# Layer 0, second half: weight buffers by place in SBUF, and the gate rows and residual loaded among the weights

## The chip, the core and the metric

The kernel runs on one core of one Trainium2 chip. TensorE (PE in the profile) multiplies, VectorE (DVE) and ScalarE (ACT) work elementwise, SyncE (SP) and GpSimd (POOL) issue the DMA transfers here. SBUF is the on-chip memory of 128 partitions in which every operand stands; PSUM takes the products. The metric is the device time of one execution in microseconds, as the median of several runs.

## The reference, cut to what matters

Two layers of a diffusion backbone over 256 context and 256 latent tokens of width 1024. A layer has a mixer (attention, SSD and retention side by side) and then a part that is called its second half here: an output projection with gated residual, a modulated RMSNorm, a squared-ReLU MLP and a gated residual. Layer 1 updates the latent tokens alone.

```python
def sq_relu_mlp(x, w1, w2):
    h = jax.nn.relu(x @ w1)          # 1024 -> 4096
    return (h * h) @ w2              # 4096 -> 1024

# merge_branches ends in: return merged @ w_out
for layer in range(DEPTH):
    mod_lat = jnp.split(jax.nn.silu(c) @ w_mod[layer] + b_mod[layer], 6, axis=-1)
    ...
    h_lat = h_lat + mod_lat[2][:, None, :] * mix_lat
    v_lat = modulate(rms_norm(h_lat, norm2_w[layer]), mod_lat[3], mod_lat[4])
    h_lat = h_lat + mod_lat[5][:, None, :] * sq_relu_mlp(v_lat, w_mlp1[layer], w_mlp2[layer])
    if need_ctx:                     # layer 0 alone: the same for the context tokens
        ...
```

All of it is in float32.

## The kernel before, in words

**Units.** A weight matrix is read in units of 128 x 1024 float32 (0.52 MB). For each, `load_w` takes a buffer `raw` and has SP load it, ScalarE casts it into `wh` (the leading part of the number, fp32r), and VectorE takes `wl = raw - wh` (`split`, under high priority). `fm` then runs 24 matmuls: for each of 8 slices of the contraction `wh` with the leading part of the activations, `wh` with their rest, and `wl` with the leading part. In layer 0 each streams 512 columns (the context and latent tokens), so a unit is 24 matmuls of 512 columns.

**Activations.** `uh` and `ul` hold the leading part and the rest of the input of the output projection and of the MLP's first matrix; they stand in pool `cp`, at the low addresses of SBUF (36 to 68 KB of a partition). The hidden layer of the MLP, `hh_` and `hl_`, stands in `hpool`, at the high addresses (142 to 206 KB).

**Weight buffers.** `wh` and `wl` come from two pools: two of each from `wp`, which follows the activations at the low addresses (86 to 103 KB), and two of each from a pool that the second half opens for itself (`wb`, from 119 KB up). `alt` takes them in turn: unit number n of the half (counted from 1) gets the pool's buffers when n is even and over 4, else `wp`'s. So four units can stand converted. The first half of layer 0 has no such second pool for `wh` and `wl` (its `w` is 0) and runs with the two of `wp` alone. `raw` has three buffers in `wp` and one in the pool.

**Order of the second half of layer 0.** Output projection: units wo0 to wo6, then wo7 in two halves of 256 columns with the norm behind each (`last_block`). Then MLP in two rounds of 16 units w1 and 16 units w2 (two for each of 8 output blocks); the first two w1 units of round one, and the last two w2 units of round two, run in halves of 256 columns. Behind each wo unit stands the residual of that block, which adds it to the old h: `h` is loaded for this in eight pieces of 0.26 MB from DRAM. The weights of the gate of the MLP's residual (`graw`, 16 pieces of 0.26 MB) are loaded in this stretch too, for the small matmuls after wo7; they lie where `hh_` will be.

**What sets the order.** The program is recorded in the order of the code; a scheduler then puts the instructions of each engine into a fixed order by dependencies and priorities. Each engine runs its list strictly in that order, and SP issues its transfers strictly in that order; a DMA waits until its buffer is free.

## Time and profile before

| | |
|---|---|
| median of three runs | 1469.29 us (1468.2 to 1469.41) |
| the profiled execution | 1468.76 us, of which its span is 1467.0 |
| TensorE | busy 1444.2 us, 98% of the span; mean granted clock 0.996 |
| VectorE, ScalarE | busy 1011.4 us (69%) and 666.0 us (45%) |
| second half of layer 0 | from 515.5 us of the span to about 951 |

Matmul records overlap, so the busy share of TensorE does not tell how dense the matmuls are; the distance between the starts of two units does. A stretch of the second half can be read from three things: how long its units take, on which engine TensorE waits, and what the DMA engines moved.

### The profile page before, as it was taken

The page shows a single profiled execution, that of the slowest core. Times are in us where ns is not written, and L with a number is a line of the kernel's source. Part 1 is how long each engine was busy: PE and PEld are TensorE (multiplying, and loading weights), DVE is VectorE, ACT ScalarE, POOL GpSimd, SP SyncE. Part 2 cuts the span into 40 slices and gives each one's busy share as a digit, 9 for nine tenths or more (in the row PEclk, how much of TensorE's full clock was granted, in tenths as well). Part 3 has the DMA queues.
Part 4 walks back from the last instruction along what each step waited for, and adds up shares of the span by engine and source line. Part 5 has one row for each costly group of instructions (what it writes and reads, how often), then busy time and mean ns, then how long its engine had stood idle before and what let it go on. Part 6 is the DMA issues. An engine that isn't in the chain of part 4 may idle for free.

```text
span 1467.0 us, 22934 instructions
## 1 busy us (share of the span) xinstructions
PE 1444.2 (98%) x8950; PEld 1243.9 (85%) x8950; DVE 1011.4 (69%) x2003; ACT 666.0 (45%) x1170; POOL 70.6 (5%) x134
## 2 busy tenths in 40 slices
PE   8999999999999979999999999999999999999997
PEld 6888877878888868888888888987988999999997
DVE  5778599588866756896456643697894886775664
ACT  4577567242322334432224322476762444663553
POOL 0000010000000020000001100000000020000000
PEclk9999999999999999999999999999999999999999
DMA  9511343455135482454445543241443456665551
GB/s 354 178 44 44 101 127 98 129 172 158 35 109 170 147 311 77 158 198 161 143 156 189 189 130 107 80 131 53 141 147 101 144 190 222 219 190 187 185 182 65
DMA packets 65085, 217.09 MB, mean 148 GB/s; under 512 B 7600, under 2 KB 10032, under 8 KB 64848
## 3 DMA queue, kind: packets, MB, share of 16 engines
q1 hardware_dynamic: 50960, 166.80, 34.5%
q0 software_dynamic: 14016, 48.83, 10.3%
q8 instruction: 70, 1.15, 0.3%
q14 instruction: 39, 0.32, 0.1%
HBM read 213.44 MB, written 2.16 MB: 147 GB/s over the span
## 4 chain that ended last, share of the span: by engine, by line
PE 88%; DVE 5%; DMA 4%; issue 2%; ACT 1%; SPq 0%; POOL 0%; DVEq 0%; POOLq 0%
PE gps L255 23%; PE gps L253 23%; PE gps L254 23%; PE mps L669 2%; PE mps L630 1%; PE mps L652 1%; DMA raw<-in_wk_dram 1%; DVE wl L223 1%; DMA raw<-in_ws_dram 1%; PE mps L952 1%; PE mps L954 1%; PE mps L953 1%; DMA h<-in_h_dram 1%; PE mps L766 1%; PE mps L976 1%
## 5 line engine op out<-in xcount | busy, mean ns | idle before, releaser
L222 ACT CAST wh<-raw 128x1024 fp32r<-128x1024 f32 (+1 forms) x284 | 297.7, 1050 | 577.3 <-PE gps L254 476.7
L223 DVE TENSOR_TENSOR wl<-raw,wh 128x1024 fp32r<-128x1024 f32 (+1 forms) x284 | 347.3, 1224 | 263.2 <-ACT wh L222 259.8
L253 PE MATMUL gps<-uh,wh 128*128 128x256 f32 (+1 forms) x1304 | 444.3, 341 | 7.0 <-ACT wh L222 6.5
L255 PE MATMUL gps<-uh,wl 128*128 128x256 f32 (+1 forms) x1304 | 444.1, 341 | 1.2 <-DVE wl L223 1.2
L254 PE MATMUL gps<-ul,wh 128*128 128x256 f32 (+1 forms) x1304 | 443.9, 341 | 0.0
L253 PEld LDWEIGHTS gps<-uh,wh 128*128 128x128 f32 x1304 | 246.9, 189 | 35.9 <-ACT wh L222 7.3
L255 PEld LDWEIGHTS gps<-uh,wl 128*128 128x128 f32 x1304 | 247.0, 189 | 29.8 <-DVE wl L223 2.8
L254 PEld LDWEIGHTS gps<-ul,wh 128*128 128x128 f32 x1304 | 247.1, 190 | 27.3 <-issue 0.9
L255 PE MATMUL gps<-hh__5379,wl 128*128 128x512 f32 (+1 forms) x272 | 103.5, 380 | 0.0
L253 PE MATMUL gps<-hh__5379,wh 128*128 128x512 f32 (+1 forms) x272 | 103.3, 380 | 0.0
L254 PE MATMUL gps<-hl__5380,wh 128*128 128x512 f32 (+1 forms) x272 | 103.2, 379 | 0.0
L216 DVE CUSTOM_DVE_ANT_0 mraw<-mraw,crow,cl 128x1024 f32<-128x1024 f32 x64 | 82.0, 1281 | 1.1
L253 PE MATMUL gps<-hh__11969,wh 128*128 128x256 f32 x256 | 72.3, 282 | 0.0
L255 PE MATMUL gps<-hh__11969,wl 128*128 128x256 f32 x256 | 72.2, 282 | 0.0
L254 PE MATMUL gps<-hl__11970,wh 128*128 128x256 f32 x256 | 72.1, 282 | 0.0
L1100 DVE SCALAR_TENSOR_TENSOR h<-gps,mod,h 128x256 f32<-128x256 f32 x48 | 21.8, 480 | 70.6 <-PE gps L255 70.6
L254 PE MATMUL gps<-brl,wh 128*128 128x512 f32 (+1 forms) x192 | 65.7, 342 | 0.0
L255 PE MATMUL gps<-brh,wl 128*128 128x512 f32 (+1 forms) x192 | 65.6, 342 | 0.0
L253 PE MATMUL gps<-brh,wh 128*128 128x512 f32 (+1 forms) x192 | 65.2, 340 | 0.0
L253 PEld LDWEIGHTS gps<-hh__5379,wh 128*128 128x128 f32 x272 | 51.2, 188 | 10.3
L254 PEld LDWEIGHTS gps<-hl__5380,wh 128*128 128x128 f32 x272 | 51.2, 188 | 10.2
L208 POOL DMA_DIRECT2D mraw<-in_wt_dram x62 | 33.4, 539 | 548.6 <-DVE mod L216 531.7
(325 smaller groups left out, 2355.4 us busy)
## 6 DMA issues: line engine op xcount, KB each, us to landing
raw<-in_ws_dram SPq DMA_DIRECT2D x280, 512.0 KB, 3.5
mraw<-in_wt_dram POOLq DMA_DIRECT2D x62, 512.0 KB, 3.6
mraw<-in_wm_dram SPq DMA_DIRECT2D x16, 512.0 KB, 9.9
graw<-in_wg_dram POOLq DMA_DIRECT2D x32, 256.0 KB, 8.0
R<-drow POOLq DMA_DIRECT2D x24, 256.0 KB, 4.4
h<-in_h_dram SPq DMA_DIRECT2D x16, 256.0 KB, 6.6
raw<-in_wk_dram SPq DMA_DIRECT2D x4, 544.0 KB, 4.9
crow<-in_cr_dram SPq DMA_DIRECT2D x1, 1024.0 KB, 10.9
```

Of the source, the lines that this page charges most:

```text
L208: (nc.sync if l == 0 and cb < 18 else nc.gpsimd).dma_start(raw, wt[WTI[l] + cb - WT0[l]])
L216: V.tensor_tensor_reduce(o, r, crow[:, v], 0.5, col(l, "bm")[:, cb:cb + 1], ALU.mult, ALU.add, mods[l][:, cb, v:v + 1])
L222: W["cp"] = A.copy(hi, src)
L223: return V.tensor_tensor(lo, src, hi.bitcast(F32), ALU.subtract)
L253: PE.matmul(ps, a, xh(k), start=start and k == 0, stop=False)
L254: PE.matmul(ps, a, xl(k), start=False, stop=False)
L255: W["mm"] = PE.matmul(ps, b, xh(k), start=False, stop=stop and k == K - 1)
L630: PE.matmul(ps[:, u * nk:u * nk + nk], qT_[:, 4 * g + j0 + u, i * 128:i * 128 + 128], kT_[:, g, x, 0:nk], start=x == 0, stop=x == 1)
L652: PE.transpose(pt[:, c * 128:c * 128 + 128], pr[:, c * 128:c * 128 + 128], ident)
L669: PE.matmul(po[64 * u:64 * u + 64, jp * 128:jp * 128 + 128], vt[:, c, 64 * g:64 * g + 64], pT[:, c, u], start=c == 0, stop=c == ncn - 1, t ...
L766: PE.matmul(ps[:, 0:256], xb[:, c, 256:384], xd, start=True, stop=True)
L1100: W["dv"] = V.scalar_tensor_tensor(h[:, i, a:b], ps[:, a - q0:b - q0], coef[:, i, v:v + 1], h[:, i, a:b], ALU.mult, ALU.add)
```

## The change

Three things are changed in the second half of layer 0. A unit's `wh` and `wl` come from `wp` alone (two sets) where it meets `uh` and `ul` (wo, w1), and from the second pool alone (two sets) where it meets `hh_` and `hl_` (w2); the same for the first projection of layer 1, by halves. The 16 gate pieces are issued by SP and no longer by GpSimd, two behind each wo unit, the last four behind wo6. The pieces of h are issued two ahead of wo0 and then one behind each of wo0 to wo5; this loop is written for both layers, while the gate pieces of layer 1 stay as they were.

```diff
-        def load_w(src, n, pool=None):
+        def load_w(src, n, pool=None, far=False):
...
                 raw = alt("raw", F32, "r", 3)
-                wh = alt("wh", F32R, "w", 2)
-                wl = alt("wl", F32R, "w", 2)
+                if W["near"]:
+                    wh, wl = [(W["pool"] if far else wp).tile([P, 1088], F32R, tag=t_, name=t_, bufs=2) for t_ in ("wh", "wl")]
+                else:
+                    wh = alt("wh", F32R, "w", 2)
+                    wl = alt("wl", F32R, "w", 2)
...
         def unit(l, *nm):
-            return load_w(ws[l, UIDX[nm]], 1024)
+            return load_w(ws[l, UIDX[nm]], 1024, far=nm[0] == "w2")
...
-                         n=0, r=1 if not last else 2, w=2)
+                         n=0, r=1 if not last else 2, w=2, near=not last)
...
-                (nc.sync if j == 8 else nc.gpsimd).dma_start(raw, wg[l, j - 20, kk, i])
+                (nc.gpsimd if l else nc.sync).dma_start(raw, wg[l, j - 20, kk, i])
...
-                for i in range(8):
+
+                def load_h(i):
                     nc.sync.dma_start(h[:, i, q0:T], (hd if l else h0)[:, i, q0:T])
 
+                for i in range(2):
+                    load_h(i)
+
                 gate = mod_rows(l, 20, 24, hpool.tile([P, 16, 4, 128], F32, tag="hh_", name="graw"))
-                for ld, _ in gate:
-                    ld()
+                if last:
+                    for ld, _ in gate:
+                        ld()
...
                 for i in range(7):
                     ps = gps(None)
                     fm(l, ("wo", i), qh, ql, 8, ps[:, 0:nq])
+                    if not last:
+                        for ld, _ in gate[2 * i:2 * i + 2 if i < 6 else 16]:
+                            ld()
+                    if i < 6:
+                        load_h(i + 2)
                     residual(i, ps, m2h, ranges)
```

ScalarE at the output projection, before: `acc` and `sq` are squares of the residual h; the casts are of wo3 (raw_5028), wo5 (raw_5100), wo7 (raw_5173), wo4 (raw_5064) and wo6 (raw_5136).

```order
L279 ACTIVATE acc_4893<-h_4894 128x512
L275 ACT_TABLE_LOAD
L222 CAST wh_5029<-raw_5028 128x1024
L285 ACTIVATE sq_4988<-h_4894 128x512
L222 CAST wh_5101<-raw_5100 128x1024
L222 CAST wh_5174<-raw_5173 128x1024
L222 CAST wh_5065<-raw_5064 128x1024
L285 ACTIVATE sq_5024<-h_4894 128x512
L222 CAST wh_5137<-raw_5136 128x1024
```

The same place in the changed program, where the casts are of wo3 (raw_5015), wo4 (raw_5054), wo5 (raw_5093), wo6 (raw_5132) and wo7 (raw_5173).

```order
L282 ACTIVATE acc_4893<-h_4894 128x512
L278 ACT_TABLE_LOAD
L222 CAST wh_5016<-raw_5015 128x1024
L288 ACTIVATE sq_4972<-h_4894 128x512
L222 CAST wh_5055<-raw_5054 128x1024
L288 ACTIVATE sq_5011<-h_4894 128x512
L222 CAST wh_5094<-raw_5093 128x1024
L288 ACTIVATE sq_5050<-h_4894 128x512
L222 CAST wh_5133<-raw_5132 128x1024
L288 ACTIVATE sq_5089<-h_4894 128x512
L222 CAST wh_5174<-raw_5173 128x1024
```

Before, the casts of wo5 and wo7 stand ahead of that of wo4; now the casts come in the order in which the units run, one between two squares.

SP's transfers at the same place, before, from wo2 (raw_4992) on: wo3, wo7, wo4, the eight pieces of h, wo5, wo6, and the first w1 unit (raw_5382). The gate pieces are on GpSimd's list.

```order
L240 DMA raw_4992<-in_ws_dram 128x1024
L240 DMA raw_5028<-in_ws_dram 128x1024
L240 DMA raw_5173<-in_ws_dram 128x1024
L240 DMA raw_5064<-in_ws_dram 128x1024
L1092 DMA h_4894<-in_h0_dram 128x512 x8
L240 DMA raw_5100<-in_ws_dram 128x1024
L240 DMA raw_5136<-in_ws_dram 128x1024
L240 DMA raw_5382<-in_ws_dram 128x1024
```

SP's transfers there in the changed program, from wo2 (raw_4976) on, with the gate pieces as `graw`.

```order
L243 DMA raw_4976<-in_ws_dram 128x1024
L243 DMA raw_5015<-in_ws_dram 128x1024
L171 DMA graw_4897<-in_wg_dram 128x512 x8
L1096 DMA h_4894<-in_h0_dram 128x512 x6
L243 DMA raw_5054<-in_ws_dram 128x1024
L171 DMA graw_4897<-in_wg_dram 128x512 x2
L1096 DMA h_4894<-in_h0_dram 128x512
L243 DMA raw_5093<-in_ws_dram 128x1024
L171 DMA graw_4897<-in_wg_dram 128x512 x2
L1096 DMA h_4894<-in_h0_dram 128x512
L243 DMA raw_5132<-in_ws_dram 128x1024
L171 DMA graw_4897<-in_wg_dram 128x512 x4
```

The scheduler has put eight gate pieces and six pieces of h in one run between the weights of wo3 and wo4; the remaining ten alternate with the weights.

## Rows read from the trace of the kernel before

**Rows 1.** The page: span, and TensorE's busy time.

```profile
span 1467.0 us, 22934 instructions
PE 1444.2 (98%) x8950; PEld 1243.9 (85%) x8950; DVE 1011.4 (69%) x2003; ACT 666.0 (45%) x1170; POOL 70.6 (5%) x134
```

**Rows 2.** Windows by stage: wo0 to wo6, four MLP stages, start of layer 1.

```profile
core 0: us, PE busy (x) PEld busy (x) DVE busy (x) ACT busy (x) POOL busy (x), PEclk, DMA share, GB/s
...
515.50:564.20 48.70, 41.28 (x170) 32.31 (x170) 25.06 (x39) 14.74 (x18) 9.77 (x18) 0.93 0.72 257
...
588.30:665.60 77.30, 77.30 (x338) 63.21 (x337) 68.55 (x95) 30.52 (x42) 6.45 (x12) 1.00 0.56 182
665.60:754.00 88.40, 88.40 (x385) 72.21 (x384) 41.16 (x57) 17.93 (x18) 4.84 (x9) 1.00 0.46 150
754.00:842.40 88.40, 88.40 (x385) 72.24 (x385) 59.69 (x81) 33.77 (x47) 8.53 (x16) 1.00 0.56 185
842.40:919.80 77.40, 77.40 (x338) 63.21 (x337) 30.45 (x40) 20.97 (x24) 3.88 (x8) 1.00 0.37 120
...
944.00:1010.00 66.00, 65.56 (x461) 56.72 (x460) 53.94 (x157) 45.04 (x95) 0.54 (x1) 1.00 0.28 89
```

**Rows 3.** Windows inside the output projection, same columns.

```profile
515.50:521.00 5.50, 5.50 (x26) 4.51 (x26) 5.50 (x11) 1.68 (x2) 4.75 (x9) 1.00 0.75 242
...
526.00:532.00 6.00, 6.00 (x27) 4.69 (x25) 1.75 (x4) 2.70 (x3) 3.17 (x6) 1.00 1.04 390
532.00:545.00 13.00, 6.09 (x25) 4.35 (x24) 4.04 (x5) 3.70 (x5) 0.00 (x0) 0.91 0.77 302
545.00:553.00 8.00, 7.49 (x24) 5.57 (x25) 5.28 (x8) 2.25 (x4) 0.00 (x0) 0.72 0.76 252
```

**Rows 4.** Waits, 515 to 565 us: total, times, longest.

```profile
ACT wh L222 <- DMA raw<-in_ws_dram: 9.3, 1, 9.3
...
PE gps L253 <- ACT wh L222: 6.5, 2, 6.2
```

**Rows 5.** Timeline, ScalarE, output projection: start, duration, instruction, idle before.

```profile
529.27 0.63 ACT L279 ACTIVATE acc<-h 128x512 f32<-128x512 f32 x1 [6.07 <-DVE h L1100]
529.92 1.28 ACT L275 ACT_TABLE_LOAD   x1
531.22 1.05 ACT L222 CAST wh<-raw 128x1024 fp32r<-128x1024 f32 x1
...
542.10 2.94 ACT L222 CAST wh<-raw 128x1024 fp32r<-128x1024 f32 x3 [9.30 <-DMA raw<-in_ws_dram]
```

**Rows 6.** The chain that ended last, 520 to 550 us: start, duration.

```profile
521.53 6.81 DMA h<-in_h_dram
...
528.40 13.68 DMA raw<-in_ws_dram
```

**Rows 7.** Timeline, ScalarE, casts in the w1 stage of round one.

```profile
604.78 1.05 ACT L222 CAST wh<-raw 128x1024 fp32r<-128x1024 f32 x1 [3.25 <-PE gps L254]
...
610.37 1.05 ACT L222 CAST wh<-raw 128x1024 fp32r<-128x1024 f32 x1 [3.37 <-PE gps L254]
...
615.83 1.05 ACT L222 CAST wh<-raw 128x1024 fp32r<-128x1024 f32 x1 [3.25 <-PE gps L254]
```

**Rows 8.** Timeline, ScalarE, casts in the w2 stage of round one.

```profile
671.20 1.06 ACT L222 CAST wh<-raw 128x1024 fp32r<-128x1024 f32 x1 [3.39 <-PE gps L254]
676.69 1.05 ACT L222 CAST wh<-raw 128x1024 fp32r<-128x1024 f32 x1 [4.42 <-PE gps L254]
682.27 1.05 ACT L222 CAST wh<-raw 128x1024 fp32r<-128x1024 f32 x1 [4.54 <-PE gps L254]
```

**Rows 9.** Timeline, VectorE, the subtraction behind the first cast of rows 7.

```profile
605.87 1.22 DVE L223 TENSOR_TENSOR wl<-raw,wh 128x1024 fp32r<-128x1024 f32 x1 [0.35 <-ACT wh L222]
```

**Rows 10.** Timeline, ScalarE, casts in the first half of layer 0.

```profile
499.00 1.05 ACT L222 CAST wh<-raw 128x1024 fp32r<-128x1024 f32 x1 [4.07 <-PE gps L254]
504.46 1.06 ACT L222 CAST wh<-raw 128x1024 fp32r<-128x1024 f32 x1 [4.40 <-PE gps L254]
```

## The prediction

> **What bounds the kernel now.** I began with the page's engine line: TensorE is busy 1444.2 of 1467.0 us [rows 1]. A gain can therefore come only from places where its units run apart or run slowly, and I looked for both with windows by stage [rows 2].

> The first place is the output projection. Its seven units wo0 to wo6 take 48.70 us, with 41.28 us of matmul and a granted clock of 0.93 [rows 2]. A unit that nothing delays takes 5.46 us: the distance of two casts in the first half of layer 0, where a cast waits for a unit of the same size to end [rows 10]. Seven of them are 38.2 us, so 48.70 - 38.2 = 10.5 us are lost here.

> The waits say on what: ScalarE waits once for 9.3 us for a transfer, and TensorE waits 6.5 us in all for a cast, one of them 6.2 us [rows 4]. ScalarE's timeline gives the place: its square of h at 529.27, a table load and one cast up to 532.27, then nothing until three casts at 542.10 [rows 5]. By its order these three are wo5, wo7 and wo4. TensorE needs wo4 next, but wo5 stands ahead of it, and SP issues wo5 behind all eight pieces of h: the chain has h from 521.53 for 6.81 us, then weights from 528.40 for 13.68 us, which land at 542.08 [rows 6]. So wo4's cast waits for a transfer that it doesn't need.

> The windows inside the stage show the price. From 526 to 532 the transfers run at 390 GB/s, the most seen here, since gates, h and weights come at once. [...] The clock's share is (1 - 0.91) x 13 + (1 - 0.72) x 8 = 3.4 us; with 6.5 of waits that is 9.9 of the 10.5. The rest lies where wo3 waits for the first square of h: VectorE had kept h back, and ScalarE stood 6.07 us for it [rows 5].

> The second place is the MLP: 14, 16, 16 and 14 units take 77.30, 88.40, 88.40 and 77.40 us [rows 2], 331.5 us for 60, or 5.525 each, with matmuls all along and a clock of 1.00. Against 5.46 that is 331.5 - 327.6 = 3.9 us. It isn't spread evenly. In w1 the casts, each let go by the end of a unit, stand 5.59 and then 5.46 apart [rows 7]; in w2 5.49 and then 5.58 [rows 8]. Counting tells which unit is slow. With eight wo units and two w1 units ahead, unit 11 starts at 588.3; so 604.78 to 610.37 is unit 14, even, in the high buffers, while `uh` and `ul` lie low. The w2 stage starts at 665.6 with unit 25; 671.20 to 676.69 is unit 26, and 676.69 to 682.27 unit 27, odd, in the low buffers, while `hh_` and `hl_` lie high. So in both stages the slow unit has its weights at the other end of SBUF from the operand that it meets.

> **The change part by part.** *Placement.* Every whole unit gets the near kind. I take 5.46 for all 60: -3.9 us. Bounds: 0, if the address has no part in the pace, and the 3.9; nothing here shows a unit below 5.46. The units in halves, five with wo7, are left at nothing; at the same 0.13 each they could hold 0.65.

> [...]

> *Two sets instead of four.* The cast of a unit now starts when the unit two before it ends, so it has one unit's time, 5.46 us. Cast 1.05, subtraction from 605.87 for 1.22: ready 2.3 us after 604.78 [rows 7, 9]. `wl` is first needed by the third matmul, 2 x 5.46/24 = 0.45 us into the unit. Slack: 5.46 + 0.45 - 2.3 = 3.6 us. VectorE is the one that could eat it: busy 68.55 of 77.30 in w1 of round one [rows 2], but the subtractions go first among its ready work. At the border from w1 to w2 the two new sets are free at once, so two subtractions more (2.4 us) fall into that stage, whose spare time is 8.75. The first half of layer 0 runs on two sets at 5.46 [rows 10]. Cost: 0; bounds 0 and what rival C says.

> *Casts and loads in order.* ScalarE's casts now come in the order of the units, so the 9.3 us wait has nothing to stand on. What is late next is a transfer. SP now has, behind wo3, eight gate pieces, six of h, and wo4; whatever holds the first gate piece or the first h holds wo4 too. wo3 is due at 515.5 + 3 x 5.46 = 531.9; before, h landed at 528.34 and wo3's cast ended at 532.27, 3.9 us later [rows 5, 6], so h must be there by 528.0. Ahead of it and with it go 8 x 0.262 + 0.52 + 0.26 = 2.9 MB. The gates need the buffer that the branches leave about when the stage starts, and h a buffer that VectorE left at 521.53 [rows 6]; I take 518 as the start of the flow, between 515.5 and 521.53. At 390 GB/s the first piece lands at 525.4, in time; at the 242 of the stage's beginning [rows 3] at 529.9, 1.9 late. For wo4 the sum is 5.24 MB: 531.4 at 390, 535.4 at 302, 539.7 at 242, and it must be there by 537.3 - 1.1 = 536.2: 0 to 3.5 late. Behind it every unit brings at most 1.57 MB, 4.0 us at 390 or 5.2 at 302, within a unit's 5.46. As a whole the stage moved 48.70 x 257 = 12.5 MB [rows 2], which in 38.2 us asks for 328 GB/s, under 390 and over 302; the same bound, some 3 us. I take 0.5 us for all this, near the low end, since the mixed flow is the one that ran at 390. The gate pieces leave GpSimd's list, where nothing of the stage waits behind them; they are wanted only after wo7.

> *Layer 1.* Its gate pieces and eight loads of h stay in one run, but the scheduler orders its beginning somewhat anew: casts of the first projection come earlier, and some of k ahead of two of weights. In 944 to 1010 TensorE is busy 65.56 of 66.00 [rows 2], so no more than 0.4 is to be had; a cast and subtraction in the way would cost 2.3. I take 0.

> *Sum.* 10.5 + 3.9 - 0.5 = 13.9 us. The profiled execution took 1468.76, which becomes 1454.9. The median of before is 1469.29, 0.5 above that execution; the forecast is 1455.4 us.

> **Rivals.** A, *the place of the buffers is nothing*: the alternation of rows 7 and 8 comes from something else that the two kinds of unit differ in. Then 10.0 remain: 1459.3. For it: nothing here changes the place alone. Against: the slow kind changes sides just where the operand does. [...]

> B, *SP's list is too slow*: the transfers run at 242, wo4 comes 3.5 late, and TensorE's idling brings the lower clock back, at the 8 x 0.28 = 2.2 us of rows 3. From 14.4, 8.7 to 10.9 us remain: 1458.4 to 1460.6. For it: the fourteen pieces between wo3 and wo4. Against: 390 GB/s for the same mixture.

> C, *two sets are too few, and it gets slower*: a subtraction or cast comes so late in w1 or w2 that TensorE waits in each unit. It decides from 13.9/67 = 0.21 us a unit (60 and the seven wo); at 0.5 the sum is +33.5 and the time 1488.9. For it: VectorE's 89% in w1. Against: it must come over 3.6 us late every time, and the half that ran on two sets held 5.46.

> That the change doesn't do what it says holds for layer 1 in part, as told; if its start loses the 2.3, the time is 1457.7.

> **How the numbers follow.** Forecast 0.70 (its own range 1453.5 to 1457.7), A 0.09, B 0.13, C 0.05, anything else, layer 1 above all, 0.03. The prediction is the likeliest case. The range from 1452.5 (the halves' 0.65, nothing late, and the 0.4 of layer 1, with a little over) to 1460.5 takes in A and most of B. No change is what lies within 0.2%, 2.9 us, about what a measurement of this kernel can tell. Forecast, A and B are all faster than that: 0.92; C is slower, 0.05; the rest may cancel, 0.03.

> **What would show it.** After, wo0 to wo6 should take 38 to 39 us at a clock near 1.00, ScalarE should have no long wait for weights there, and casts should stand 5.46 apart in w1 and in w2 alike, the four stages taking 76.4, 87.4, 87.4 and 76.4 us. Pace at 5.59 that stays, or falls on all units, is A; a wait of TensorE for wo3 or wo4 with a transfer behind it is B; waits of TensorE for `wh` or `wl` in every MLP unit is C. The forecast is wrong if the stages keep their lengths, or if what they give back is lost again after 944.

## The result and the profile after

The changed kernel takes 1451.9 us (median, 1451.12 to 1455.12) against 1469.26 before: a ratio of 0.9889, interval 0.9877 to 0.9901, 17.4 us. That is faster, as forecast, by more than the 13.9 us of the sum; the median lies 0.6 us below the range of 1452.5 to 1460.5. The profiled execution took 1455.12, so the traces account for 1468.76 - 1455.12 = 13.6 us.

The page of the changed kernel, in answer to [rows 1]:

```profile
span 1453.4 us, 22908 instructions
PE 1437.6 (99%) x8950; PEld 1244.5 (86%) x8950; DVE 1011.2 (70%) x2003; ACT 665.2 (46%) x1170; POOL 61.9 (4%) x118
```

Windows by stage of the changed kernel, in answer to [rows 2]: wo0 to wo6, the four MLP stages, the start of layer 1.

```profile
core 0: us, PE busy (x) PEld busy (x) DVE busy (x) ACT busy (x) POOL busy (x), PEclk, DMA share, GB/s
...
518.10:556.20 38.10, 38.10 (x169) 31.47 (x168) 22.77 (x35) 12.86 (x15) 1.08 (x2) 1.00 0.82 304
580.30:656.50 76.20, 76.20 (x338) 63.12 (x337) 69.36 (x96) 31.70 (x43) 6.46 (x12) 1.00 0.57 193
656.50:743.60 87.10, 87.10 (x386) 72.13 (x385) 41.08 (x57) 17.86 (x18) 4.85 (x9) 1.00 0.47 152
743.60:830.60 87.00, 87.00 (x385) 72.04 (x384) 59.52 (x81) 33.65 (x46) 8.60 (x16) 1.00 0.57 187
830.60:906.80 76.20, 76.20 (x338) 63.08 (x337) 31.51 (x41) 21.88 (x25) 3.80 (x7) 1.00 0.37 123
938.00:1000.00 62.00, 61.59 (x423) 52.53 (x423) 53.61 (x157) 45.78 (x99) 0.54 (x1) 1.00 0.33 104
```

Read each against its row of before: the output projection 48.7 to 38.1, 10.6 us less; the MLP stages 77.3, 88.4, 88.4, 77.4 to 76.2, 87.1, 87.0, 76.2, 5.0 less. From the start of wo7 to that of the third w1 unit both take 24.1 us. From the end of the last whole w2 unit to the end of the span it was 1467.0 - 919.8 = 547.2 and is 1453.4 - 906.8 = 546.6, 0.6 less. That is 16.2; the second half of layer 0 began at 515.5 before and at 518.1 after, 2.6 later, and 16.2 - 2.6 = 13.6 closes the account.

The 2.6 us belong to the first half, where both programs have the same instructions in the same order. Some 1.7 of them stand at the start, most of it in this window of the changed kernel:

```profile
20.00:25.00 5.00, 4.51 (x28) 4.03 (x21) 3.68 (x11) 2.07 (x5) 0.00 (x0) 0.66 1.05 397
```

The granted clock is 0.66 there as a mean, and 0.50 from 22 to 24 us. The engine had been busy 3.93 of the 5 us before; before the change, with 3.72 of 5, the same window shows 1.00. A second trace of the changed kernel (after_again, below) has 1.00 there, its second half starts at 514.7, and its span is 1450.0. So the profiled execution was the longest of the four, and the median is 3.2 us below it.

ScalarE in the output projection of the changed kernel, in answer to [rows 5]:

```profile
530.25 0.63 ACT L282 ACTIVATE acc<-h 128x512 f32<-128x512 f32 x1 [4.49 <-DVE h L1108]
530.90 1.28 ACT L278 ACT_TABLE_LOAD   x1
532.19 1.05 ACT L222 CAST wh<-raw 128x1024 fp32r<-128x1024 f32 x1
533.14 0.63 ACT L288 ACTIVATE sq<-h 128x512 f32<-128x512 f32 x1
535.29 1.05 ACT L222 CAST wh<-raw 128x1024 fp32r<-128x1024 f32 x1 [1.52 <-DMA raw<-in_ws_dram]
...
539.93 1.05 ACT L222 CAST wh<-raw 128x1024 fp32r<-128x1024 f32 x1 [3.05 <-PE gps L257]
```

The wait of 9.30 us is gone. wo4's cast (535.29) waits 1.52 us for its transfer and is done at 536.3; TensorE starts wo4 at 539.9. wo3's cast ends at 533.24 for a unit that starts at 534.47. Its subtraction follows, from 533.27 for 1.23 us, and the third matmul, the first to need it, starts at 534.92: 0.4 us, the least that the stage has to spare.

Casts of the changed kernel in w1, then in w2, in answer to [rows 7, 8]:

```profile
602.08 1.05 ACT L222 CAST wh<-raw 128x1024 fp32r<-128x1024 f32 x1 [3.22 <-PE gps L257]
607.52 1.06 ACT L222 CAST wh<-raw 128x1024 fp32r<-128x1024 f32 x1 [3.23 <-PE gps L257]
612.96 1.06 ACT L222 CAST wh<-raw 128x1024 fp32r<-128x1024 f32 x1 [3.23 <-PE gps L257]
...
689.13 1.06 ACT L222 CAST wh<-raw 128x1024 fp32r<-128x1024 f32 x1 [4.39 <-PE gps L257]
694.57 1.05 ACT L222 CAST wh<-raw 128x1024 fp32r<-128x1024 f32 x1 [4.38 <-PE gps L257]
700.01 1.05 ACT L222 CAST wh<-raw 128x1024 fp32r<-128x1024 f32 x1 [4.39 <-PE gps L257]
```

Every unit takes 5.44 us, less than the 5.46 that the sum took as the best.

### The profile page after: what moved, and what is told of

It reads as the page before. It is cut to its first block, busy times and chain, and to the rows that moved or that the text cites. A ratio compares the mean times of both kernels' runs of the same rounds, so it can differ in the third digit from the quotient of the medians.

```text
span 1453.4 us, 22908 instructions
## 1 busy us (share of the span) xinstructions
PE 1437.6 (99%) x8950; PEld 1244.5 (86%) x8950; DVE 1011.2 (70%) x2003; ACT 665.2 (46%) x1170; POOL 61.9 (4%) x118
## 4 chain that ended last, share of the span: by engine, by line
PE 92%; DVE 3%; issue 3%; ACT 1%; DMA 1%; POOL 0%; DVEq 0%; POOLq 0%; ACTq 0%
PE gps L256 24%; PE gps L257 24%; PE gps L258 23%; PE mps L672 2%; PE mps L633 1%; PE mps L655 1%; PE mps L955 1%; PE mps L957 1%; PE mps L956 1%; DVE wl L223 1%; PE mps L769 1%; PE mps L979 1%; DMA R<-drow 1%; PE mps L352 1%; PE mps L351 1%
## 5 line engine op out<-in xcount | busy, mean ns | idle before, releaser
L258 PE MATMUL gps<-hh__5379,wl 128*128 128x512 f32 (+1 forms) x272 | 102.6, 377 | 0.0
L258 PEld LDWEIGHTS gps<-hh__5379,wl 128*128 128x128 f32 x272 | 51.2, 188 | 9.3
```

The costliest lines, as they stand in the source:

```text
L258: W["mm"] = PE.matmul(ps, b, xh(k), start=False, stop=stop and k == K - 1)
```

## The experiments

All are edits of the changed kernel unless told otherwise. A unit below is one of 512 columns.

### The two parts apart

**place_only** keeps the near buffers and puts the loads back:

```diff
-                (nc.gpsimd if l else nc.sync).dma_start(raw, wg[l, j - 20, kk, i])
+                (nc.sync if j == 8 else nc.gpsimd).dma_start(raw, wg[l, j - 20, kk, i])
...
-                for i in range(2):
+                for i in range(8):
                     load_h(i)
...
-                if last:
-                    for ld, _ in gate:
-                        ld()
+                for ld, _ in gate:
+                    ld()
...
-                    if not last:
-                        for ld, _ in gate[2 * i:2 * i + 2 if i < 6 else 16]:
-                            ld()
-                    if i < 6:
-                        load_h(i + 2)
```

> The two near sets of weight buffers as in the change; the gate pieces on GpSimd and the eight pieces of h in one run, as before. With two sets the scheduler puts ScalarE's casts in the order of the units (wo4, wo5, wo6, wo7), though SP still issues wo5 behind all of h. Theory 1 (the stall came from the order of the casts): wo4 is no longer held, only wo5 is late by the transfer that landed 26.6 us after the stage began, about 1.3 us; wo0 to wo6 take 39 to 40 us, the four MLP stages 76.2, 87.1, 87.1 and 76.2, and the time is 1 to 2 us above the changed kernel. Rival (the stall came from the transfers, gates and h in front of weights): wo0 to wo6 keep 46 to 49 us, and the time is 8 to 10 us above the changed kernel.

It took 1454.22 us, 0.9901 of before (0.9886 to 0.9915). Its windows of wo0 to wo6 and of the first MLP stage, and ScalarE's casts of wo3, wo4 and wo5:

```profile
516.30:556.00 39.70, 38.67 (x169) 31.31 (x168) 22.76 (x35) 12.74 (x15) 9.77 (x18) 1.00 0.79 288
580.10:656.30 76.20, 76.20 (x338) 63.08 (x337) 69.31 (x96) 31.70 (x43) 6.46 (x12) 1.00 0.59 193
```

```profile
532.22 1.05 ACT L222 CAST wh<-raw 128x1024 fp32r<-128x1024 f32 x1
533.17 0.63 ACT L288 ACTIVATE sq<-h 128x512 f32<-128x512 f32 x1
533.70 1.03 ACT L222 CAST wh<-raw 128x1024 fp32r<-128x1024 f32 x1
...
542.42 1.05 ACT L222 CAST wh<-raw 128x1024 fp32r<-128x1024 f32 x1 [5.84 <-DMA raw<-in_ws_dram]
```

wo5 still lands at 542.4, yet the stage takes 39.7 us: 9.0 of the 10.6 come back with the loads as they were. With two sets there is no buffer free for an early cast of wo5 or wo7, so wo4 stands ahead. The 1.6 us that remain are not where the expectation had them. wo5 is in time; TensorE waits at wo3, whose cast comes behind the first square of h, and that square waited for h:

```profile
532.42 0.39 PE L258 MATMUL gps<-uh,wl 128*128 128x512 f32 x1
533.32 0.50 PE L256 MATMUL gps<-uh,wh 128*128 128x512 f32 x1 [0.51 <-ACT wh L222]
533.65 0.40 PE L257 MATMUL gps<-ul,wh 128*128 128x512 f32 x1
534.58 0.50 PE L258 MATMUL gps<-uh,wl 128*128 128x512 f32 x1 [0.53 <-DVE wl L223]
```

**loads_only** keeps the loads and takes the weight buffers in turn from both pools again:

```diff
-                         n=0, r=1 if not last else 2, w=2, near=not last)
+                         n=0, r=1 if not last else 2, w=2, near=False)
```

> The loads as in the change; weight buffers in turn from both pools, four sets, as before. Theory 1: the casts stand in the order of the units here too, so wo0 to wo6 take 38 to 39 us; the MLP stages keep 77.3, 88.4, 88.4 and 77.4 us, so the time is about 5 us above the changed kernel. If the pace of 5.44 came from the loads and not from the place, the stages would be 76.2, 87.1, 87.1 and 76.2 and the time that of the changed kernel.

1459.97 us, 0.9941 (0.9924 to 0.9957). Its output projection, and its first two MLP stages:

```profile
516.30:554.60 38.30, 38.30 (x170) 31.50 (x169) 25.07 (x37) 14.63 (x18) 1.07 (x2) 1.00 0.90 328
578.70:656.00 77.30, 77.30 (x338) 63.20 (x337) 68.56 (x95) 30.53 (x43) 6.45 (x12) 1.00 0.56 182
656.00:744.40 88.40, 88.40 (x385) 72.22 (x384) 41.14 (x57) 17.92 (x18) 4.85 (x9) 1.00 0.47 150
```

The stages are as expected; the time is 8 us above the changed kernel and not 5. Of the 7.9 by which its trace is longer than that of after_again, 5.0 are the MLP, 1.7 are there before the second half begins, and 1.0 lies between w2 and the branches of layer 1. Either part alone puts the casts of wo in order and saves most of the stall, so the two savings don't add; the pace of the MLP comes with the buffers alone.

### Is it the end of SBUF?

**far** has two sets too, each from the other pool (`if far` becomes `if not far`); **mixed** takes only wl from the other pool (`if far != (t_ == "wl")`).

> As the changed kernel with two sets, but the sides changed: wh and wl from the high pool where they meet uh and ul, from wp where they meet hh_ and hl_. Theory 1 (a weight at the other end slows each matmul of 512 columns): every whole unit takes 5.59, so wo0 to wo6 39.1 us, the MLP stages 78.3, 89.4, 89.4 and 78.3, some 10 us more than the changed kernel in all. Rival (the alternation came from four sets in two pools, not from the place): all stages as in the changed kernel.

Single times: far 1463.98 us, mixed 1461.61. Two MLP stages of far:

```profile
578.90:657.30 78.40, 78.40 (x339) 63.09 (x338) 70.01 (x97) 31.67 (x43) 6.47 (x12) 1.00 0.58 188
657.30:746.90 89.60, 89.60 (x386) 72.09 (x385) 40.45 (x55) 17.85 (x18) 4.86 (x9) 1.00 0.46 147
```

5.60 a unit, with two sets as in the changed kernel, so the number of sets is not the reason.

> As the changed kernel, but wl at the other end: of each three matmuls two have near weights and one far ones. If each matmul's own weights set its pace: (2 x 226.7 + 232.7)/3 = 228.7 ns, 5.49 us a unit. If a running matmul is slowed by the loading of the next one's weights: the same mean, but the slow one is the second of the three, while wl is loaded. If the worse of the two decides for the unit: 5.59.

TensorE in mixed, one round of three matmuls and the next one's start, with the load (PEld) of wl:

```profile
607.36 0.40 PE L257 MATMUL gps<-ul,wh 128*128 128x512 f32 x1
607.36 0.19 PEld L258 LDWEIGHTS gps<-uh,wl 128*128 128x128 f32 x1
607.59 0.40 PE L258 MATMUL gps<-uh,wl 128*128 128x512 f32 x1
607.83 0.39 PE L256 MATMUL gps<-uh,wh 128*128 128x512 f32 x1
608.05 0.40 PE L257 MATMUL gps<-ul,wh 128*128 128x512 f32 x1
```

The unit takes 5.55 us: none of the three expectations. From start to start, over the 28 whole w1 units from 585 us on, a matmul of uh with wh takes 226.8 ns, the next, of ul with wh, 232.6, and that of uh with wl 234.1. So one far weight slows two matmuls, the one during which it is loaded and its own. The change from one kind of unit to the other also tells why the near units of before took 5.46 and not 5.44: in the one from 610.41 the first three matmuls, behind a far unit, took 228, 233 and 230 ns, and the last, ahead of the next one, 232.

**border** asks where the border between the ends lies. It moves wp up behind tp and takes every weight of layer 0's second half from wp:

```diff
+        tp = ctx.enter_context(tc.tile_pool(name="tp", bufs=2))
         wp = ctx.enter_context(tc.tile_pool(name="wp", bufs=2))
...
-        tp = ctx.enter_context(tc.tile_pool(name="tp", bufs=2))
...
+        wp.tile([P, D], F32, tag="mraw", name="mraw", bufs=MB)
         th = tp.tile([P, 8, 2], F32, tag="sm", name="th")
...
-                    wh, wl = [(W["pool"] if far else wp).tile([P, 1088], F32R, tag=t_, name=t_, bufs=2) for t_ in ("wh", "wl")]
+                    wh, wl = [wp.tile([P, 1088], F32R, tag=t_, name=t_, bufs=2) for t_ in ("wh", "wl")]
```

> The changed kernel with wp moved up behind tp, all wh and wl of layer 0's second half from wp, two sets: wh at 102.6 and 106.9 KB, wl at 111.1 and 115.4 KB, each 4.25 KB long, uh and ul at 36.8 to 68.8, hh_ and hl_ at 142.9 to 206.9. If the distance between weights and operand sets the pace, uh meets them at about the distance at which wp met it and runs at 226.7 ns, and hh_ at a pace between 226.7 and 234. If there is a border, matmuls on one side of it are fast with uh and slow with hh_, on the other side the reverse; the allocations reach up to 224 KB, and a border in the middle, at 112, would make wh fast with uh and slow with hh_, wl at 115.4 slow with uh and fast with hh_, and wl at 111.1 would change at its second slice.

A single time of 1468.07 us, since wp serves uh and ul in the first halves of both layers too: the first half of layer 0 ends 5.4 us later than in after_again. Its casts in w1, then in w2:

```profile
605.59 1.05 ACT L223 CAST wh<-raw 128x1024 fp32r<-128x1024 f32 x1 [3.35 <-PE gps L258]
611.17 1.06 ACT L223 CAST wh<-raw 128x1024 fp32r<-128x1024 f32 x1 [3.36 <-PE gps L258]
...
694.01 1.06 ACT L223 CAST wh<-raw 128x1024 fp32r<-128x1024 f32 x1 [4.38 <-PE gps L258]
699.45 1.06 ACT L223 CAST wh<-raw 128x1024 fp32r<-128x1024 f32 x1 [4.38 <-PE gps L258]
```

All of uh is slow (5.58) and all of hh_ fast (5.44), for wh and wl alike. wh at 102.6 KB is slow with uh here; wl at 99.0 to 103.0 KB is fast with uh in the changed kernel. Only a border within 0.1 KB of 103.0 could explain both, and the runs of the next section leave that one no room either. hh_ and hl_ moved down in this build, to 125.9 KB, which the expectation had not reckoned with. What all runs so far share stands in the addresses that the build assigned (bytes within a partition):

```
                     start                          modulo 256   with uh/ul   with hh_/hl_
uh, ul               37632, 54016                   0
hh_, hl_             146304, 179072                 128
hh_, hl_ in border   128896, 161664                 128
wp                   88320, 92672, 97024, 101376    0            fast         slow
high pool            126848, 131200, 135552 ...     128          slow         fast
wp in border         105088, 109440, 113792 ...     128          slow         fast
```

Modulo 512 the four buffers of wp differ among themselves (256 and 0), and all are fast with uh; so 256 is enough.

### The remainder of the address

**same_alt**, **same_far** and **other_near** test that by themselves: a unit's 1024 columns may begin later in its buffer of 1088. In same_alt (four sets in turn, as before) and same_far (buffers as in far) they begin 128 bytes later where the remainders would differ; in other_near (near buffers) they are made to differ. The core of same_alt, where `hi` says that the buffers are the high pool's:

```diff
+            if want is not None:
+                o = (want - (128 if hi else 0)) % 256 // 4
+                wh, wl = wh[:, o:o + n], wl[:, o:o + n]
...
+        def want(l, nm):
+            return {"wo": 0, "w1": 0, "w2": 128}.get(nm[0]) if l == 0 else None
...
-            return load_w(ws[l, UIDX[nm]], 1024, far=nm[0] == "w2")
+            return load_w(ws[l, UIDX[nm]], 1024, far=nm[0] == "w2", want=want(l, nm))
...
-                         n=0, r=1 if not last else 2, w=2, near=not last)
+                         n=0, r=1 if not last else 2, w=2, near=False)
```

> New theory (remainder): the pace depends on the start addresses of weights and streamed operand modulo 256 bytes, not on the end of SBUF. uh and ul have remainder 0, hh_ and hl_ 128, wp's weight buffers 0, the high pool's 128; at 512 columns a matmul is fast where the two agree. In the run border, wp's buffers moved to 102.6 KB and remainder 128, and uh, still near, ran at 233 ns. Here the loads are as in the change, the weight buffers four sets in turn from both pools as before, but a unit's 1024 columns begin 128 bytes later in the buffer where the remainders would differ. Remainder: all four MLP stages at 5.44 a unit, 76.2, 87.1, 87.1 and 76.2 us, the time that of the changed kernel, 1450 to 1455 us. Place (the prediction's reason): the far half of the units stays at 5.59, stages 77.3, 88.4, 88.4 and 77.4, some 5 us more.

> As the run far (weights always from the other end, two sets), but each unit begins 128 bytes later in its buffer, so that its remainder agrees with that of the operand. Remainder: 5.44 us a unit, stages 76.2, 87.1, 87.1 and 76.2. Place: 5.60 a unit, stages 78.4, 89.6, 89.6 and 78.4, as in far.

> As the changed kernel (near, two sets), but the units begin later in their buffers: wo by 128 bytes, w1 by 64, w2 by 32. Remainder: wo at 5.57 to 5.60 us a unit; w1 and w2 at 5.60 if any difference modulo 256 counts, w2 at 5.44 if only 64 bytes or more do, both at 5.44 if only 128 does. Place: all at 5.44.

same_alt: 1453.33 us, 0.9892 (0.9877 to 0.9907). Single times: same_far 1455.35, other_near 1462.53. The first two MLP stages of each, same_alt first:

```profile
579.50:655.70 76.20, 76.20 (x338) 63.07 (x338) 68.43 (x95) 30.63 (x43) 6.45 (x12) 1.00 0.57 185
655.70:742.70 87.00, 87.00 (x386) 72.03 (x384) 41.27 (x57) 17.90 (x19) 4.85 (x9) 1.00 0.50 152
```

same_far, whose buffers are those that ran at 5.60 in far:

```profile
579.70:655.90 76.20, 76.20 (x338) 63.09 (x337) 69.18 (x96) 31.70 (x43) 6.45 (x12) 1.00 0.58 193
655.90:743.00 87.10, 87.10 (x386) 72.11 (x385) 41.27 (x57) 17.85 (x18) 4.85 (x9) 1.00 0.47 152
```

other_near, whose buffers are those of the changed kernel:

```profile
578.40:656.80 78.40, 78.40 (x338) 62.92 (x337) 70.04 (x97) 31.66 (x43) 6.45 (x12) 1.00 0.60 188
656.80:746.40 89.60, 89.60 (x386) 72.25 (x385) 40.44 (x57) 17.80 (x18) 4.85 (x9) 1.00 0.47 147
```

In these runs the place is nothing and the remainder all: with equal remainders the MLP units of the far ends and of the four sets run at 5.44, and with 64 bytes of difference (w1) or 32 (w2) the near ones run at 5.60. The output projection of same_alt took 39.1 us at the same pace of matmuls, since its wo3 waited for wl.

### Versions that might be faster

**far1** and **far1_four** came before the remainder was understood. They put layer 1, whose units stream 256 columns, at the other end, where the trace has 2.84 us a unit against 2.88:

```diff
-                    wh, wl = [(W["pool"] if far else wp).tile([P, 1088], F32R, tag=t_, name=t_, bufs=2) for t_ in ("wh", "wl")]
+                    wh, wl = [(W["pool"] if far != W["last"] else wp).tile([P, 1088], F32R, tag=t_, name=t_, bufs=2) for t_ in ("wh", "wl")]
...
-                         n=0, r=1 if not last else 2, w=2, near=not last)
+                         n=0, r=1 if not last else 2, w=2, near=True, last=last)
```

far1_four has four sets instead of two for wo and w1 of layer 1.

> The changed kernel, and in the second half of layer 1, whose matmuls stream 256 columns, the opposite placement: wh and wl of wo and w1 from the high pool (two sets), of w2 from wp (two sets). In the changed kernel's trace far units take 2.84 us there and near ones 2.88, in turn. If being far helps at 256 columns, all 72 units come to 2.80 to 2.84 us: 1.4 to 4.3 us less than the changed kernel. If the alternation itself gives the 2.84, all come to 2.88 and it is 1.4 us slower. If two sets are too few for units of 2.88 us (cast and subtraction take 2.3), it is slower by more, with waits of TensorE for wh and wl.

> As far1, but with four sets in the high pool for wo and w1 of layer 1 (w2 keeps two in wp). 1.4 to 4.3 us less than the changed kernel if being far helps; if far1 waits for casts in wo and w1, those waits are gone here.

> The changed kernel once more, on the chip on which the others of this call run: 1450 to 1455 us, with a first half of layer 0 that ends within 3 us of its earlier time, and stages after it as before.

after_again: 1451.54 us, 0.9883 (0.9869 to 0.9896); its first half ends 3.4 us earlier than in the first trace, a little more than the 3 expected. far1: 1461.51, 0.995 (0.9936 to 0.9963); far1_four: 1463.75, 0.9965 (0.9952 to 0.9978). Both lose some 10 us instead of winning. TensorE's waits in far1 from wo of layer 1 on, which after_again does not have:

```profile
PE gps L258 <- DVE wl L223: 3.8, 6, 0.9
PE gps L256 <- ACT wh L222: 1.5, 2, 1.1
```

The two waits for wh stand at wo0, whose buffers come from the pool that the second half opens. Layer 1's output projection takes 30.4 us against 28.2 of after_again, 2.1 of the 2.2 in its first unit; it also starts 2.4 us later, of which 1.2 are there when the second half of layer 0 begins. What follows takes 199.2 us against 194.2. The six waits for wl lie there, and five of them stand at a border between w1 and w2. In far1's program the casts of the first two w2 units stand among those of the last three of w1, the first ahead of all three and the second ahead of two, since the two kinds no longer share buffers; ScalarE waits with each of the two for a transfer. In the first round, where hh_ starts at 1310.6, `x2` is the cast that waited and the one behind it:

```profile
1297.20 2.00 ACT L222 CAST wh<-raw 128x1024 fp32r<-128x1024 f32 x2 [1.26 <-DMA raw<-in_ws_dram]
...
1301.54 2.00 ACT L222 CAST wh<-raw 128x1024 fp32r<-128x1024 f32 x2 [1.62 <-DMA raw<-in_ws_dram]
```

TensorE then waits for wl at 1300.69 and 1305.05. So this is the stall of the output projection again, and not rival C: most units of 2.85 us run on two sets without a wait. The order alone does not do it: far1_four has the same order of casts with four sets for w1, and there no wait is left ahead of w2; what follows its output projection takes 195.0 us. That output projection takes 35.8; why it is so much longer was not followed further. The changed kernel has two w2 casts among the last two w1 ones in layer 0 too, where units take 5.44 us, and TensorE does not wait there.

The pace itself came out as hoped: at 256 columns the matmuls of far1 stand 118.3 to 118.8 ns apart in w2, where the changed kernel has 118.3 and 120.0 in turn.

**resid** sets remainders by width: equal for the branch units of 512 columns, unequal for units of 256.

```diff
+        def want(l, nm):
+            if l == 0:
+                if nm in (("wo", 7), ("w1", 0), ("w1", 1)):
+                    return 128
+                if nm[:3] == ("w2", 1, 7):
+                    return 0
+                return {"wo": 0, "w1": 0, "w2": 128, "br": 160}.get(nm[0])
+            return {"wo": 128, "w1": 128, "w2": 0, "g": 128}.get(nm[0])
```

> The changed kernel with remainders set by the width: in layer 0 the branch units of 512 columns begin 160 bytes later (brh and brl have remainder 160, their weights 0, and ran at 234 ns): 288 matmuls x 7 ns = 2.0 us less. Units of 256 columns are made to differ (near ones with equal remainders ran at 120.0 ns, with unequal ones at 118.5): in layer 1 some 35 units of MLP and output projection and those of the gates, 24 x 1.5 ns = 0.04 us each, 1 to 3 us in all. Remainder: 3 to 5 us less than the changed kernel, 1447 to 1449 us. Place: no change, since nothing moves to another end.

1450.21 us, 0.9876 (0.9858 to 0.9894): below the changed kernel's 1451.54, but the intervals overlap, and the two were not timed beside each other. The 3 to 5 us expected did not come. Its trace has the second half of layer 0 starting 1.3 us earlier than after_again, of the 2.0 expected (the branch matmuls stand 227 to 230 ns apart instead of 234), and is 1.2 us shorter behind that. It has the lowest time of all, by less than can be told apart.

## Why the prediction was right, and where not

**The stall: right in size, in part right in cause.** 10.5 us were forecast, 10.6 came. The prediction had wo4's cast behind that of wo5 for nearly all of it. place_only, with the casts in order and the loads as they were, brings back 9.0; the other 1.6 stand at wo3, behind the late h, for which the prediction left 0.6. Its clock term of 3.4 us is worked out from the 0.91 and 0.72 of [rows 3]: the trace of before has a granted clock of 0.50 from 543 to 549 us, with matmuls of 512 columns 427 ns apart instead of 227 between 547.3 and 549.0, and the changed kernel has 1.00 in the whole stage. The prediction also told the order of the casts together with the new loads and gave the two sets no part in it; place_only shows that two sets alone put the casts in order, loads_only (10.4 us back) that the loads alone do.

**The lateness of the loads: 0.5 charged, none found.** The stage took 7 x 5.44 = 38.1 us. From 523.6 to 545.4 the transfers ran at 364 to 411 GB/s, near the 390 of the prediction's better case, and wo4's weights came in time. Rival B did not happen. It would have begun at wo3, which had 0.4 us to spare.

**Two sets instead of four: right.** The casts of w1 and w2 wait for TensorE (3.2 and 4.4 us each), not TensorE for them. In units half as long two sets are too few at the borders of w1 and w2, as far1 shows: five of its six waits for wl (3.8 us for the six) stand there.

**The placement: right in sign, too small, wrong in cause.** 3.9 us were forecast, 5.0 came. The mis-sized term is the reference of 5.46 us. The unit of [rows 10] comes behind one of brh, at 234 ns a matmul, and its own first two matmuls took 233 and 231 ns before the pace fell to 226.7. Among equal units it is 5.44, and 60 x 0.02 = 1.2 is about the missing 1.1. The reason given, the other end of SBUF, is refuted: same_far and other_near show the remainder of the address modulo 256 instead. The change was right by luck: wp happens to share its remainder with uh and ul, and the high pool with hh_ and hl_. Rival A, that the place is nothing, was true to the letter, and its time was wrong all the same, since the change of buffers also made the remainders equal.

In mixed the matmul that ran while a weight with another remainder was loaded took 232.6 ns instead of 226.8, so there the load was not free for it; what stands behind that no run shows.

**Layer 1: 0.6 us less** behind the last whole w2 unit, a little beyond the bound of 0.4. **The rest of the 17.4** of the medians is some 1.2 us above the 16.2 that the stages of the traces give. No run assigns it; the first halves of the two traces of the changed kernel alone differ by 3.4 us (518.1 and 514.7).

## What to carry to other kernels

Before a pace is put down to a region of memory, compare the operands' addresses by remainder: a shift by a few columns inside the buffer tests it without moving anything else. Take the reference pace from a run of equal units, not from one whose neighbours are slow. And more sets of buffers are no gift to an engine with a fixed order: here they let casts run ahead that then stood in front of the one that was due, for 9.3 us. Separate sets for two kinds of unit can do the same where the kinds change, as in far1.
